# A two-layer MLP by seven products: the first two pairs of up projections interleaved, and the first down loads issued among the last up products

## The chip, the cores and the metric

One NeuronCore of a Trainium2 chip runs the whole program. The metric is device time in microseconds (us), from one launch. TensorE (PE) multiplies, VectorE (DVE), ScalarE (ACT) and GpSimd (POOL) do elementwise work, and the queue of SyncE (SP) issues most DMAs.

## What is computed

The reference is one step of a decoder trunk with two layers. Layer 0 is a pair of state space mixers, layer 1 an attention with three branches, and each layer ends in the same MLP. It runs on 1024 prompt tokens and 8 x 4 sample tokens, 1056 in all:

```python
x += relu(RMSNorm(x) @ w_up)^2 @ w_down      # 1024 -> 4096 -> 1024, once per layer
```

Only the two MLPs are touched. All values are float32.

## The kernel before, in words

**The two MLPs.** Function mlp (L1298) runs once per layer, first on the output of the mixers, then on that of the attention. It has an up stage and a down stage, which follow each other in `R[0], r = W["raw"], ...` to the end of mlp (from L1552).

**Seven products for eight.** Weights and input are each cut into two by two blocks, and a block product is found from seven products p1 to p7 instead of eight (PROD, L1358). p1, p2 and p3 multiply blocks of the input (b11, b21, b22); p5, p6, p7 and p4 multiply sums of blocks (t1, t2, t3, t4). On the weight side a11, a12 and a22 are blocks, s1 to s4 sums of blocks, and p3 uses the sum s4. So p3 has a block of the input but a sum of the weights.

**Split operands.** Each float32 operand is split in two parts, hi and lo. ACT casts hi, DVE subtracts it for lo, and three matmuls (L1372 to L1374, L1513 to L1515) take the place of one. b_split (L1228) splits one input block of 528 columns, prep (L1319) one weight block or sum of 512, two_of (L1423) the operands of down. A product for one pair of weights is 2 column halves x 4 row blocks x 3 = 24 matmuls of 264 columns.

**Up.** There are 16 pairs of weight tiles (index p). up_raw (L1287) loads the raw weights of a pair by two DMAs on SP; sums (L1303) forms s1 to s4 on POOL (L1315); prep splits. The blocks of the input of the first two rows (q = 0, 1) are split and summed while the stage before still runs; those of q = 2, 3 at the start of mlp: b_sum (L1236) forms t1 on DVE and t3, t2, t4 on POOL (L1242), in place in the tiles of the input. The program writes all splits and sums first, then the products of pair 0 (p1, p2, p5, p6, p7, p4), then for each further pair p1, p3 of the pair before, p6, p2, p7, p5, p4. After each product of pair p the weight of the same product of pair p+1 is prepared.

**Evacuation.** p1, p6, p7 and p4 add up in one PSUM bank for each column half (tag A), copied out by ACT after p1, p6 and p7 (L1377) and p4 (L1380). p5 and p3 add up in B, p2 is in C. DVE adds the copies and the banks (L1384, L1388, L1392) and applies relu and square (L1344). t_sums (L1349) forms the sums for down, and everything is stored to DRAM by DMAs on SP (keep, L1339).

**Down.** For each of seven products, 16 steps of 24 matmuls. ready (L1434) issues the loads for one step, a_load (L1409, raw weights) and b_load (L1417, h from DRAM), and the splits. down (L1519) calls ready for three steps before the first and for step i+2 in step i. Before, the first three calls stand behind all products of up.

**What sets the order.** The order in which the program is written is a priority. A scheduler at build time puts each instruction on its engine's queue when, by its own timing, the operands are ready and a buffer is free. Each engine and each queue then works in that order. Buffers are given by tag, with a fixed number each, in the order of the program: "h" 8 (weight sums, raw down weights, p4's copy), "x" 5 (splits of input and of h, t sums), "wh" 4 and "sw" 2 (split weights), "w" 2 and "wr" 2 (raw up weights of even and odd pairs), "e" 12 (evacuated tiles). h tiles of down go to "sw", "w", "wr" in turn (BUF, L1414).

**The sums of squares.** ms_tok (L339) ends the stage before with nine thin matmuls (L343); up starts behind them.

Of the kernel before, what the change touches and what calls it, by code (L numbers as in the profile page):

```python
# [7 lines left out]
F32 = mybir.dt.float32  # L8
# [4 lines left out]
OP = mybir.AluOpType  # L13
# [180 lines left out]
def _build(ctx, nc, tc, ins, outs, dbg):  # L194
    cp = ctx.enter_context(tc.tile_pool(name="consts", bufs=1))
    sp = ctx.enter_context(tc.tile_pool(name="slots", bufs=1))
    phase, psum = [], []
# [18 lines left out]
    cnt = [0]  # L216
# [5 lines left out]
    def wslot(dt, name, tag, bufs):  # L222
        cnt[0] += 1
        return sp.tile([128, 1088], dt, name=f"{name}{cnt[0]}", tag=tag, bufs=bufs)

    def ptile(dt, name, tag, bufs, n=SLOT):

        cnt[0] += 1
        return phase[-1][1].tile([128, n], dt, name=f"{name}{cnt[0]}", tag=tag, bufs=bufs)
# [183 lines left out]
    for c in range(3):  # L413
        cc = slice(c * CH, (c + 1) * CH)
        p = px()
# [812 lines left out]
    def b_split(W, n, q, al=slot):  # L1228

        t, x = al(F32R, "xw"), part(W, n, q)  # L1230
        hi, lo = t[:, :HF], t[:, HF:NT]
        S.copy(hi, x)
        V.tensor_tensor(lo, x, hi.bitcast(F32), OP.subtract)  # L1233
        W["x"][n, q] = hi, lo
# [52 lines left out]
    def up_raw(l, p):  # L1287

        o = []
        for i in range(2):  # L1290
            t = wslot(F32, "wu", "w", 2) if p % 2 == 0 else ptile(F32, "wu", "wr", 2, 1024)
            nc.sync.dma_start(t[:, :1024], ins[f"w_up{l}"][2 * p + i])
            o.append(t[:, :1024].rearrange("p (q k f) -> p k q f", k=2, f=128))
        return o
# [3 lines left out]
    def mlp(l, W, acc, finish, hook=None):  # L1298
# [4 lines left out]
        def sums(p, n):  # L1303

            if (p, n) in SF:
                return SF[p, n]
            (a11, a12), (a21, a22) = [[r[:, k] for k in range(2)] for r in R[p]]
            if n in ("s2", "s4"):
                sums(p, "s1" if n == "s2" else "s2")
            o = half(F32, "sf")  # L1310
            ov = o.rearrange("p (q f) -> p q f", f=128)
            f = lambda k: SF[p, k].rearrange("p (q f) -> p q f", f=128)
            x, y, op = {"s1": lambda: (a21, a22, OP.add), "s2": lambda: (f("s1"), a11, OP.subtract),
                        "s3": lambda: (a11, a21, OP.subtract), "s4": lambda: (a12, f("s2"), OP.subtract)}[n]()
            nc.gpsimd.tensor_tensor(ov, x, y, op)  # L1315
            SF[p, n] = o
            return o

        def prep(p, i):  # L1319

            n = ORDER[i]
            t = wslot(F32R, "sw", "wh", 4) if i < 4 else ptile(F32R, "sw", "sw", 2, 1024)
            hi, lo = t[:, :512], t[:, 512:1024]
            x = sums(p, n) if n[0] == "s" else R[p][int(n[1]) - 1][:, int(n[2]) - 1]
            v = (lambda z: z) if n[0] == "s" else (lambda z: z.rearrange("p (q f) -> p q f", f=128))
            S.copy(v(hi), x)  # L1326
            V.tensor_tensor(v(lo), x, v(hi).bitcast(F32), OP.subtract)
            SW[p, n] = hi, lo

        def e_t():  # L1330
            return ptile(F32, "e", "e", 12, 264)

        def bank(tag, bufs):
            cnt[0] += 1
            return psum[-1][1].tile([128, 512], F32, name=f"{tag}{cnt[0]}", tag=tag, bufs=bufs)[:, :264]

        E = {}

# [3 lines left out]
        def act(x, n, p, c):  # L1342

            V.scalar_tensor_tensor(x, x, 0.0, x, op0=OP.max, op1=OP.mult)  # L1344
            E[p, c, n] = x
            if n != "b12":
                keep(n, p, c, x)

        def t_sums(p, c):  # L1349
# [4 lines left out]
            for n, o, x, y in (("t1", t1, b12, b11), ("t3", b12, b22, b12), ("t2", t2, b22, t1), ("t4", t4, b21, t2)):  # L1354
                V.tensor_tensor(o, x, y, OP.subtract)
                keep(n, p, c, o)

        PROD = {"p1": ("a11", "b11", "A", 1, 0), "p6": ("s2", "t2", "A", 0, 0), "p7": ("s3", "t3", "A", 0, 0),  # L1358
                "p4": ("a22", "t4", "A", 0, 1), "p5": ("s1", "t1", "B", 1, 0), "p3": ("s4", "b22", "B", 0, 1),
                "p2": ("a12", "b21", "C", 1, 1)}  # L1360

        def prod(p, n):
            wn, xn, bk, first, last = PROD[n]
            for c in range(2):
                if first:
                    E[p, c, bk] = bank(bk, 3 if bk == "A" else 2)
                o = E[p, c, bk]
                wh, wl = SW[p, wn]
                for q in range(4):
                    xh, xl = (t[:, c * 264:(c + 1) * 264] for t in W["x"][xn, q])  # L1370
                    a, b = (t[:, q * 128:(q + 1) * 128] for t in (wh, wl))
                    T.matmul(o, a, xh, start=bool(first and q == 0), stop=False, skip_group_check=True)  # L1372
                    T.matmul(o, a, xl, start=False, stop=False, skip_group_check=True)  # L1373
                    T.matmul(o, b, xh, start=False, stop=(q == 3), skip_group_check=True)  # L1374
                if n in ("p1", "p6", "p7"):
                    E[p, c, n] = e_t()
                    S.copy(E[p, c, n], o)  # L1377
                if n == "p4":
                    x = half(F32, "c21")[:, :264]
                    S.copy(x, o)  # L1380
                    act(x, "b21", p, c)
                if n == "p2":
                    x = E.pop((p, c, "p1"))
                    V.tensor_tensor(x, x, o, OP.add)  # L1384
                    act(x, "b11", p, c)
                if n in ("p5", "p7") and (p, c, "B") in E and (p, c, "p7") in E:
                    x = E[p, c, "p7"]
                    V.tensor_tensor(x, x, E[p, c, "B"], OP.add)  # L1388
                    act(x, "b22", p, c)
                if n == "p3":  # L1390
                    x = E.pop((p, c, "p6"))
                    V.tensor_tensor(x, x, o, OP.add)  # L1392
                    act(x, "b12", p, c)
                    t_sums(p, c)
                if last:
                    E.pop((p, c, bk))
            del SW[p, wn]
            if n == "p3":
                del R[p]
            if n == "p5":  # L1400
                prep(p, 6)
            if p < 15 and n != "p3":
                prep(p + 1, ORDER.index(wn))
# [5 lines left out]
        def a_load(i, k, q):  # L1409
# [1 line left out]
            nc.sync.dma_start(t, ins[f"w_dn{l}"][(2 * i + k) * 16 + q])  # L1411
            return t

        BUF = ((lambda: ptile(F32, "br", "sw", 2, 1024)), (lambda: wslot(F32, "br", "w", 2)),  # L1414
               (lambda: ptile(F32, "br", "wr", 2, 1024)))

        def b_load(n, q, o=0, m=HF):  # L1417
            cnt[0] += 1
# [85 lines left out]
        def step(n, q, ops, cs=(0, 1)):  # L1504
            (wh, wl), (xh, xl) = ops
            for dp in range(4):
                a, b = (t[:, dp * 128:(dp + 1) * 128] for t in (wh, wl))
                for c in cs:
# [7 lines left out]
                    if q == 15:  # L1516
                        evac(n, dp, c, o)

        def down():  # L1519
            ks = [(n, q) for n in ("p1", "p5", "p6", "p7", "p3", "p2") + (() if l else ("p4",)) for q in range(16)]  # L1520
            ops = {}
            for i, k in enumerate(ks):
                if k == ("p5", 0):
                    st["r2"] = bcast_tok(r, "r2", xslot(F32, "r2"))
                for z in ([0, 1, 2] if i == 0 else [i + 2]):
                    if z < len(ks):
                        ops[z] = ready(*ks[z])
                step(*k, ops.pop(i))
                after(*k)

                if k[0] in ("p3", "p2", "p4") and (k[1] % 2 or k[0] == "p4"):
                    for _ in range(2 if k[0] == "p4" and k[1] < 4 else 1):
                        if todo:
                            done(todo.pop(0))
# [16 lines left out]

        R[0], r = W["raw"], W["r"]  # L1552
        new_psum("up")
        prep(0, 0)
        sums(0, "s2")
        for q in (2, 3):
            b_split(W, "b11", q, xslot)
        for q in (2, 3):
            b_split(W, "b21", q, xslot if q == 2 else slot)
        prep(0, 2)  # L1560
        for q in (2, 3):
            b_split(W, "b22", q, xslot if q == 2 else slot)
        for q in (2, 3):
            b_sum(W, q, ("t1",), V)
        for n in ("t1", "t3", "t2"):
            if n == "t1":
                for q in (2, 3):
                    b_sum(W, q, ("t3", "t2", "t4"))
            for q in range(4):
                b_split(W, n, q)  # L1570
            prep(0, {"t1": 4, "t3": 1, "t2": 3}[n])
        for q in range(4):
            b_split(W, "t4", q)
        W["a"].clear()
        prep(0, 5)
        V.reciprocal(r, r)
        V.tensor_tensor(r, r, W["m1"], OP.mult)
        R[1] = up_raw(l, 1)
        for n in ("p1", "p2", "p5", "p6", "p7", "p4"):
            prod(0, n)  # L1580
        for p in range(1, 16):
            if p < 15:
                R[p + 1] = up_raw(l, p + 1)
            for n in ("p1", None, "p6", "p2", "p7", "p5", "p4"):
                prod(*((p, n) if n else (p - 1, "p3")))
        prod(15, "p3")
        W["x"].clear()
        new_psum("dn")
# [934 lines left out]
```

## Time and profile before

| | us |
|---|---|
| median of 3 runs | 3127.24 |
| lowest and highest run | 3126.2 and 3130.1 |
| profiled execution | 3129.79 |
| its span, first to last instruction | 3128.0 |
| first MLP, up: first matmul, end | 730.33, about 1075.4 |
| second MLP, up: first matmul, end | 2429.79, about 2774.5 |

The profile is of one execution. Its pages and views give busy time by engine, matmul counts in stretches with the clock that TensorE was granted (1.00 is 2.4 GHz, 0.50 is 1.2 GHz), and each engine's instructions in order of time, with the idle time ahead of one and what ended it. Matmuls overlap: one lasts about 0.28 us, while in a full stretch one starts every 0.12 us. Operations of DVE and ACT overlap a little too, so start-to-start times are used.

### The profile page before, as it was taken

How to read it: one execution, taken by the hardware profiler on the slowest of the kernel's cores; microseconds unless marked ns; L12 is line 12 of the kernel's file. 1: busy time of each engine (PE TensorE's matmuls, PEld its weight loads, DVE VectorE, ACT ScalarE, POOL GpSimd, SP SyncE). 2: the span in 40 equal slices, each digit the busy share in tenths (PEclk: the TensorE clock that was granted, in tenths of full speed). 3: DMA queues.
4: the chain of work that ended last, by engine and by line, in shares of the span. 5: the costliest groups of instructions: out<-in, count | busy, mean ns of one | idle time of the engine just before them, and what ended most of it. 6: DMA issues, size and time to landing. Idle time of an engine off the chain costs nothing. (4 is left out here: it accounts for less than half of the span.)

```text
span 3128.0 us, 58908 instructions
## 1 busy us (share of the span) xinstructions
PE 2970.6 (95%) x22228; PEld 2798.3 (89%) x22228; DVE 2204.7 (70%) x4618; ACT 1412.5 (45%) x2920; POOL 662.9 (21%) x659
## 2 busy tenths in 40 slices
PE   7999998998999999999999989999989899999998
PEld 5999886898999999999999877777869899999998
DVE  5778787778777666866223778777766877757687
ACT  4224565433333344453226666656662433334343
POOL 0000000014222001241001343434332422200133
PEclk8999999998999999999999999999999899999999
DMA  5254444522444584676532121221134344467565
GB/s 187 88 136 136 106 138 118 160 104 96 143 142 146 176 287 130 202 248 192 155 89 76 18 66 45 39 56 38 27 83 137 106 149 144 141 218 244 150 222 159
DMA packets 301285, 414.30 MB, mean 132 GB/s; under 512 B 81012, under 2 KB 202071, under 8 KB 300935
## 3 DMA queue, kind: packets, MB, share of 16 engines
q1 hardware_dynamic: 264640, 340.87, 35.8%
q0 software_dynamic: 20800, 45.43, 5.8%
q10 hardware_dynamic: 15558, 24.22, 2.1%
q8 instruction: 175, 2.87, 0.4%
q14 instruction: 112, 0.91, 0.1%
HBM read 283.81 MB, written 118.18 MB: 129 GB/s over the span
## 5 line engine op out<-in xcount | busy, mean ns | idle before, releaser
L1514 PE MATMUL dn<-xb,sb 128*128 128x264 f32 x1664 | 473.0, 287 | 2.6 <-DVE xb L1427 2.6
L1515 PE MATMUL dn<-xb,sb 128*128 128x264 f32 x1664 | 468.2, 285 | 0.0
L1513 PE MATMUL dn<-xb,sb 128*128 128x264 f32 x1664 | 455.3, 286 | 12.9 <-ACT xb L1426 10.5
L1513 PEld LDWEIGHTS dn<-xb,sb 128*128 128x128 f32 x1664 | 306.8, 189 | 13.5 <-ACT xb L1426 10.9
L1514 PEld LDWEIGHTS dn<-xb,sb 128*128 128x128 f32 x1664 | 315.1, 189 | 3.5 <-DVE xb L1427 3.4
L1515 PEld LDWEIGHTS dn<-xb,sb 128*128 128x128 f32 x1664 | 316.0, 190 | 0.0
L1372 PE MATMUL A<-xw,sw 128*128 128x264 f32 x1024 | 294.8, 289 | 15.9 <-ACT sw L1326 8.5
L1373 PE MATMUL A<-xw,sw 128*128 128x264 f32 x1024 | 294.5, 288 | 3.4 <-DVE xw L1233 3.4
L1374 PE MATMUL A<-xw,sw 128*128 128x264 f32 x1024 | 293.5, 287 | 0.0
L2243 POOL TENSOR_SCALAR P<-P,s,gates 128x640 f32<-128x640 f32 (+7 forms) x256 | 212.2, 843 | 281.0 <-DVE s L2239 231.9
L381 PE MATMUL mm<-xh,wh 128*128 128x352 f32 x672 | 225.4, 336 | 8.1 <-ACT xh L432 7.0
L382 PE MATMUL mm<-xl,wh 128*128 128x352 f32 x672 | 223.4, 333 | 5.3 <-DVE xl L433 5.2
L383 PE MATMUL mm<-xh,wh 128*128 128x352 f32 x672 | 222.6, 331 | 0.0
L2261 DVE TENSOR_TENSOR PT<-px,PT 128x512 fp32r<-128x512 f32 x264 | 177.1, 683 | 53.5 <-ACT PT L2260 52.8
L1372 PEld LDWEIGHTS A<-xw,sw 128*128 128x128 f32 x1024 | 195.6, 192 | 17.5 <-ACT sw L1326 9.0
L2285 PE MATMUL pv<-PT,vs 128*128 128x512 f32 x528 | 195.8, 439 | 11.7 <-ACT PT L2260 6.7
L1373 PEld LDWEIGHTS A<-xw,sw 128*128 128x128 f32 x1024 | 195.4, 191 | 4.1 <-DVE xw L1233 4.1
L2235 ACT ACTIVATE P<-sc,m 128x640 f32<-128x640 f32 (+7 forms) x256 | 180.1, 713 | 41.5 <-DVE m L2229 31.2
L2260 ACT CAST PT<-px 128x512 fp32r<-128x512 f32 x264 | 152.6, 594 | 98.3 <-PE px L2271 97.3
L1374 PEld LDWEIGHTS A<-xw,sw 128*128 128x128 f32 x1024 | 196.1, 192 | 0.0
L2215 PE MATMUL sc<-KT,qt 128*128 128x256 f32 x1216 | 193.6, 298 | 0.0
L2229 DVE TENSOR_REDUCE m<-sc 128x1 f32<-128x640 f32 (+7 forms) x176 | 167.0, 949 | 30.9 <-PE sc L2215 26.9
(652 smaller groups left out, 8465.6 us busy)
## 6 DMA issues: line engine op xcount, KB each, us to landing
ar<-i_w_dn SPq DMA_DIRECT2D x256, 256.0 KB
wu<-i_w_up SPq DMA_DIRECT2D x64, 512.0 KB
br<-h0t_d SPq DMA_DIRECT2D x64, 264.0 KB
wr<-i_w_in_e POOLq DMA_DIRECT2D x26, 512.0 KB, 4.5
h0t_d<-ts SPq DMA_DIRECT2D x96, 132.0 KB
br<-h0b_d SPq DMA_DIRECT2D x48, 264.0 KB
h1t_d<-ts SPq DMA_DIRECT2D x96, 132.0 KB
br<-h1b_d SPq DMA_DIRECT2D x48, 264.0 KB
```

What stands on the lines that cost most here:

```text
L381: T.matmul(o, wh, xh, start=(j == 0), stop=False)
L382: T.matmul(o, wh, xl, start=False, stop=False)
L383: T.matmul(o, wl, xh, start=False, stop=(j == n - 1))
L1372: T.matmul(o, a, xh, start=bool(first and q == 0), stop=False, skip_group_check=True)
L1373: T.matmul(o, a, xl, start=False, stop=False, skip_group_check=True)
L1374: T.matmul(o, b, xh, start=False, stop=(q == 3), skip_group_check=True)
L1513: T.matmul(o, a, h, start=(q == 0), stop=False)
L1514: T.matmul(o, a, g, start=False, stop=False)
L1515: T.matmul(o, b, h, start=False, stop=(q == 15))
L2215: T.matmul(p[:, c:c + n], w_, t, start=first, stop=True, skip_group_check=True)
L2243: nc.gpsimd.tensor_scalar(P, P, b["s"][:, h:h + 1], GT[:, qb, gc:gc + 1], op0=OP.mult, op1=OP.mult)
L2285: T.matmul(PV[g, qb, i], v, t, start=(a == 0 and kb == 0 and k == 0), stop=False)
```

## The change

At the start of up, pair 1's raw weights are loaded first, and the products of pairs 0 and 1 alternate, written out by hand: p1, p2, p3 of pair 0, the same of pair 1, then p5, p6, p7 and p4, each of both pairs. The splits and sums stand between them, each ahead of the product that needs it. For these two pairs weight sums run on DVE, and all sums of the input's blocks at q = 2, 3 run on DVE. p3 of these pairs has a bank of its own and is copied out by ACT; DVE adds copy and bank after p6. Pair 2's weights are prepared before p7 and p4 of these pairs end; from pair 2 on the order is as before. The banks are four of tag A and four that B and C share, the evacuated tiles are 15. The row factors r are inverted later.

At the end of up, ready is called for the first three steps of down, ahead of p7, p5 and p4 of pair 15. The splits of the input are let go after their last product, and h tiles take the buffers "w", "wr", "sw" in turn.

```diff
-            nc.gpsimd.tensor_tensor(ov, x, y, op)
+            (V if p < 2 else nc.gpsimd).tensor_tensor(ov, x, y, op)
...
-            return ptile(F32, "e", "e", 12, 264)
+            return ptile(F32, "e", "e", 15, 264)
...
-            return psum[-1][1].tile([128, 512], F32, name=f"{tag}{cnt[0]}", tag=tag, bufs=bufs)[:, :264]
+            return psum[-1][1].tile([128, 512], F32, name=f"{tag}{cnt[0]}", tag=tag, bufs=4)[:, :264]
...
             wn, xn, bk, first, last = PROD[n]
+            if p < 2 and n == "p3":
+                bk, first = "C", 1
             for c in range(2):
                 if first:
-                    E[p, c, bk] = bank(bk, 3 if bk == "A" else 2)
+                    E[p, c, bk] = bank("A" if bk == "A" else "B")
...
-                if n in ("p1", "p6", "p7"):
+                if n in ("p1", "p6", "p7") or p < 2 and n == "p3":
                     E[p, c, n] = e_t()
                     S.copy(E[p, c, n], o)
...
+                if p < 2 and n == "p6":
+                    x = E.pop((p, c, "p6"))
+                    V.tensor_tensor(x, x, E.pop((p, c, "p3")), OP.add)
+                    V.tensor_tensor(x, x, E[p, c, "B"], OP.add)
+                    act(x, "b12", p, c)
...
             del SW[p, wn]
+            if p == 15:
+                for q in range(4):
+                    del W["x"][xn, q]
...
-        BUF = ((lambda: ptile(F32, "br", "sw", 2, 1024)), (lambda: wslot(F32, "br", "w", 2)),
-               (lambda: ptile(F32, "br", "wr", 2, 1024)))
+        BUF = ((lambda: wslot(F32, "br", "w", 2)), (lambda: ptile(F32, "br", "wr", 2, 1024)),
+               (lambda: ptile(F32, "br", "sw", 2, 1024)))
...
+R[1] = up_raw(l, 1)
 prep(0, 0)
-sums(0, "s2")
 for q in (2, 3): b_split(W, "b11", q, xslot)
 for q in (2, 3): b_split(W, "b21", q, xslot if q == 2 else slot)
 prep(0, 2)
+prod(0, "p1")
+for n in ("s1", "s2", "s4"): sums(0, n)
+prep(0, 6)
 for q in (2, 3): b_split(W, "b22", q, xslot if q == 2 else slot)
+prod(0, "p2"); prep(1, 0); prod(0, "p3"); prep(1, 2)
+for n in ("s1", "s2", "s4"): sums(1, n)
+prep(1, 6); prod(1, "p1")
 for q in (2, 3): b_sum(W, q, ("t1",), V)
+for q in range(4): b_split(W, "t1", q)
+prep(0, 4); prod(1, "p2"); prep(1, 4); prod(1, "p3")
-(t3, t2, t4 of q = 2, 3 on POOL; splits of t1, t3, t2, t4; then up_raw(l, 1) and all products of pair 0)
+for q in (2, 3): b_sum(W, q, ("t3", "t2"), V)
+for q in range(4): b_split(W, "t2", q)
+prod(0, "p5"); prep(0, 1); prep(1, 1); prod(1, "p5"); prep(0, 3)
+for q in range(4): b_split(W, "t3", q)
+prod(0, "p6"); prep(1, 3); prep(0, 5); prod(1, "p6")
+for q in (2, 3): b_sum(W, q, ("t4",), V)
+for q in range(4): b_split(W, "t4", q)
+prep(1, 5); R[2] = up_raw(l, 2)
+prod(0, "p7"); prep(2, 0); prep(2, 1); prod(1, "p7"); prep(2, 2); prep(2, 3)
+prod(0, "p4"); prod(1, "p4"); prep(2, 4); prep(2, 5)
-for p in range(1, 16):
+for p in range(2, 16):
...
             for n in ("p1", None, "p6", "p2", "p7", "p5", "p4"):
-                prod(*((p, n) if n else (p - 1, "p3")))
+                if p == 15 and n in ("p7", "p5", "p4"):
+                    z = ("p7", "p5", "p4").index(n)
+                    ops[z] = ready(*ks[z])
+                if n:
+                    prod(p, n)
+                elif p > 2:
+                    prod(p - 1, "p3")
```

(The start is written here with several calls on a line, and one line in brackets stands for the old order.)

## Rows read from the trace of the kernel before

**Rows 1.** The page's first part: busy us, share of the span, instructions.
```profile
PE 2970.6 (95%) x22228; PEld 2798.3 (89%) x22228; DVE 2204.7 (70%) x4618; ACT 1412.5 (45%) x2920; POOL 662.9 (21%) x659
```

**Rows 2.** Windows, PE alone: stretch and length, busy (matmuls), granted clock, DMA share, GB/s.
```profile
730.33:770.00 39.67, 29.67 (x185) 0.78 0.17 57
770.00:1060.00 290.00, 290.00 (x2382) 1.00 0.45 144
2429.79:2470.00 40.21, 30.47 (x190) 0.79 0.11 35
...
1070.00:1100.00 30.00, 23.17 (x176) 0.89 0.90 286
2770.00:2800.00 30.00, 25.85 (x187) 0.89 0.88 295
1100.00:1130.00 30.00, 30.00 (x248) 1.00 0.67 211
```

**Rows 3.** Timeline of PE, start of up: start, us, instruction [idle before <- releaser].
```profile
745.19 0.59 PE L1372 MATMUL A<-xw,sw 128*128 128x264 f32 x1 [4.79 <-ACT sw L1326]
...
762.32 0.59 PE L1372 MATMUL A<-xw,sw 128*128 128x264 f32 x1 [1.90 <-ACT e L1377]
```

**Rows 4.** Waits, 730 to 770: total us, times, longest.
```profile
ACT xw L1232 <- POOL xa L1242: 8.5, 3, 5.6
```

**Rows 5.** Timeline of POOL, start of the first up.
```profile
721.64 1.29 POOL L1315 TENSOR_TENSOR sf<-wu,wu 128x512 f32<-128x512 f32 x1 [0.46 <-DVE acc L1207]
...
732.19 9.95 POOL L1315 TENSOR_TENSOR sf<-wu 128x512 f32<-128x512 f32 x1 [7.01 <-DMA wu<-i_w_up]
...
746.27 5.20 POOL L1242 TENSOR_TENSOR xa<-xa,xa 128x528 f32<-128x528 f32 x3
```

**Rows 6.** Timeline of DVE: input splits during and after that POOL operation.
```profile
738.47 2.55 DVE L1233 TENSOR_TENSOR xw<-xa,xw 128x528 fp32r<-128x528 f32 x4
...
748.73 3.32 DVE L1233 TENSOR_TENSOR xw<-xa,xw 128x528 fp32r<-128x528 f32 x2 [0.15 <-ACT xw L1232]
```

**Rows 7.** Windows of 2 us: PE, PEld, DVE, ACT, POOL busy (counts), granted clock, DMA share, GB/s.
```profile
732.00:734.00 2.00, 2.00 (x11) 2.00 (x11) 2.00 (x5) 2.00 (x5) 1.81 (x1) 0.50 0.94 380
...
750.00:752.00 2.00, 2.00 (x11) 2.00 (x10) 2.00 (x3) 1.42 (x3) 2.00 (x2) 0.50 0.00 0
```

**Rows 8.** Timeline of PE: two neighbours at the lower clock.
```profile
732.33 0.42 PE L1372 MATMUL C<-xw,sw 128*128 128x264 f32 x1
732.55 0.42 PE L1373 MATMUL C<-xw,sw 128*128 128x264 f32 x1
```

**Rows 9.** Timeline of DVE: neighbours of 264 columns.
```profile
771.25 0.43 DVE L1355 TENSOR_TENSOR e<-e,e 128x264 f32<-128x264 f32 x1
771.59 0.43 DVE L1355 TENSOR_TENSOR ts<-e,ts 128x264 f32<-128x264 f32 x1
```

**Rows 10.** Groups by line, DVE, 730.33 to 770: count, busy, mean ns, idle before.
```profile
L1233 DVE TENSOR_TENSOR xw<-xa,xw 128x528 fp32r<-128x528 f32 x21 | 19.6, 963 | 3.3 <-ACT xw L1232 3.2
```

**Rows 11.** Timeline of SP's queue at the end of the first up.
```profile
1063.21 7.66 SPq L1340 DMA_DIRECT2D h0b_d<-e  x4
...
1072.28 0.43 SPq L1411 DMA_DIRECT2D ar<-i_w_dn  x1
1072.80 1.32 SPq L1420 DMA_DIRECT2D br<-h0b_d  x1
```

**Rows 12.** Timeline of ACT, same place.
```profile
1081.02 0.62 ACT L1426 CAST sb<-ar 128x512 fp32r<-128x512 f32 x1 [1.93 <-DMA ar<-i_w_dn]
1081.54 1.70 ACT L1426 CAST xb<-br 128x528 fp32r<-128x528 f32 x3
```

**Rows 13.** Timeline of PE: first matmuls of the two down stages.
```profile
1082.22 2.13 PE L1513 MATMUL dn<-xb,sb 128*128 128x264 f32 x8 [6.83 <-ACT xb L1426]
...
2778.17 1.23 PE L1513 MATMUL dn<-xb,sb 128*128 128x264 f32 x8 [3.63 <-ACT xb L1426]
```

**Rows 14.** Timeline of DVE: the last p3 of the first up taken from its bank.
```profile
1077.19 0.42 DVE L1392 TENSOR_TENSOR e<-e,B 128x264 f32<-128x264 f32 x1
```

More of the change, by code (lines that the diff above doesn't have):

```diff
@@ L1330, in e_t, with bank @@
         def e_t():
-            return ptile(F32, "e", "e", 12, 264)
-        def bank(tag, bufs):
+            return ptile(F32, "e", "e", 15, 264)
+        def bank(tag):
             cnt[0] += 1
-            return psum[-1][1].tile([128, 512], F32, name=f"{tag}{cnt[0]}", tag=tag, bufs=bufs)[:, :264]
+            return psum[-1][1].tile([128, 512], F32, name=f"{tag}{cnt[0]}", tag=tag, bufs=4)[:, :264]
         E = {}
@@ L1381, in prod @@
                     act(x, "b21", p, c)
+                    if p < 2:
+                        t_sums(p, c)
                 if n == "p2":
@@ L1385, in prod @@
                     act(x, "b11", p, c)
+                if p < 2 and n == "p6":
[3 more added lines that the diff above has]
+                    act(x, "b12", p, c)
                 if n in ("p5", "p7") and (p, c, "B") in E and (p, c, "p7") in E:
-                    x = E[p, c, "p7"]
+                    x = E.pop((p, c, "p7"))
                     V.tensor_tensor(x, x, E[p, c, "B"], OP.add)
                     act(x, "b22", p, c)
-                if n == "p3":
+                    if p < 2:
+                        E.pop((p, c, "B"))
+                if p >= 2 and n == "p3":
                     x = E.pop((p, c, "p6"))
@@ L1397, in prod @@
             del SW[p, wn]
+            if p == 15:
+                for q in range(4):
+                    del W["x"][xn, q]
+            if p < 2:
+                return
             if n == "p3":
@@ L1517, in step @@
                         evac(n, dp, c, o)
+        ks = [(n, q) for n in ("p1", "p5", "p6", "p7", "p3", "p2") + (() if l else ("p4",)) for q in range(16)]
+        ops = {}
         def down():
-            ks = [(n, q) for n in ("p1", "p5", "p6", "p7", "p3", "p2") + (() if l else ("p4",)) for q in range(16)]
-            ops = {}
             for i, k in enumerate(ks):
@@ L1525, in down @@
                 for z in ([0, 1, 2] if i == 0 else [i + 2]):
-                    if z < len(ks):
+                    if z < len(ks) and z not in ops:
                         ops[z] = ready(*ks[z])
@@ L1560, in mlp @@
         prep(0, 2)
+        prod(0, "p1")
+        for n in ("s1", "s2", "s4"):
+            sums(0, n)
+        prep(0, 6)
         for q in (2, 3):
             b_split(W, "b22", q, xslot if q == 2 else slot)
+        prod(0, "p2")
+        prep(1, 0)
+        prod(0, "p3")
+        prep(1, 2)
+        for n in ("s1", "s2", "s4"):
+            sums(1, n)
+        prep(1, 6)
+        prod(1, "p1")
         for q in (2, 3):
             b_sum(W, q, ("t1",), V)
[L1565 to L1571, printed above, removed]
+        for q in range(4):
+            b_split(W, "t1", q)
+        prep(0, 4)
+        prod(1, "p2")
+        prep(1, 4)
+        prod(1, "p3")
+        for q in (2, 3):
+            b_sum(W, q, ("t3", "t2"), V)
+        for q in range(4):
+            b_split(W, "t2", q)
+        prod(0, "p5")
+        prep(0, 1)
+        prep(1, 1)
+        prod(1, "p5")
+        prep(0, 3)
+        for q in range(4):
+            b_split(W, "t3", q)
+        prod(0, "p6")
+        prep(1, 3)
+        prep(0, 5)
+        prod(1, "p6")
+        for q in (2, 3):
+            b_sum(W, q, ("t4",), V)
         for q in range(4):
@@ L1574, in mlp @@
         W["a"].clear()
-        prep(0, 5)
+        prep(1, 5)
+        R[2] = up_raw(l, 2)
+        prod(0, "p7")
+        prep(2, 0)
+        prep(2, 1)
+        prod(1, "p7")
+        prep(2, 2)
+        prep(2, 3)
+        prod(0, "p4")
         V.reciprocal(r, r)
         V.tensor_tensor(r, r, W["m1"], OP.mult)
-        R[1] = up_raw(l, 1)
-        for n in ("p1", "p2", "p5", "p6", "p7", "p4"):
-            prod(0, n)
-        for p in range(1, 16):
+        prod(1, "p4")
+        del R[0], R[1]
+        prep(2, 4)
+        prep(2, 5)
+        for p in range(2, 16):
             if p < 15:
```

## The prediction

> **What bounds the kernel now.** The page's first part comes first: PE is busy for 95% of the span [rows 1], so time can only be won where PE stands or runs slow, and the place of each stretch counts, not a share. Next, a windows view of PE alone [rows 2]. In the middle of the up stage of the first MLP 2382 matmuls take 290.00 us, 0.1217 us each, which I take for the second MLP too. Around that, four stretches are thinner. From the first up matmul at 730.33 to 770 there are 185 matmuls, 183 of them up products (two belong to the row sums): at 0.1217 they need 22.3 us of the 39.67, so 17.4 are lost. In the second MLP 190 matmuls need 23.1 of 40.21 us: 17.1 lost. Where up hands over to down, 176 and 187 matmuls lie in 30 us, where the down stage a little later has 248 (0.121 each): 8.7 and 7.4 us lost. Together 50.6 us; all that the change can return lies in there.
>
> What ends the idle times at the start is read on PE's timeline [rows 3]: 4.79 us until ACT's cast of a weight tile, 1.90 until an evacuation. Those casts stand in ACT's queue behind casts of the sums t3, t2 and t4, which wait for POOL: 8.5 us in three waits [rows 4]. POOL's timeline says why it is late [rows 5]: a weight sum that takes 1.29 us with little beside it lasted 9.95 us from 732.19, with DVE at work back to back, and the block sums after it took some 1.7 each (three in 5.20). DVE pays as well [rows 6]: four splits of 528 columns took 2.55 us (0.64 each) while that one stood, two took 3.32 (1.66 each) beside the sums after it. So the start hangs on POOL and DVE hindering each other, while PE has pair 0 alone to work on. Each pause has a price behind it: at a granted clock of 0.50 (1.2 GHz) [rows 7], matmuls start 0.22 us apart [rows 8], 0.098 more than at full clock.
>
> **The change, part by part: the start.** Pairs 0 and 1 alternate: p1, p2, p3 of each need only block splits of the input, then p5, p6, p7, p4, which need t1 to t4. That gives PE 2 x 3 x 24 = 144 matmuls (17.5 us) before the first t, where now it has 48 of p1 and p2 and then p5. All t sums of the last two rows of blocks and all weight sums of pairs 0 and 1 go to DVE. Off POOL: six block sums and eight weight sums per MLP. Does DVE carry it? I count its work from the first matmul to p6 of pair 2, the first product that needs a POOL sum. Large operations: 5 splits of b11, b21, b22; 8 weight sums; 8 block sums; 16 splits of t; 12 weight splits: 49 x 0.64 = 31.4. Small ones of 264 columns, which start 0.34 us apart [rows 9]: p2 two, p6 three (one more than now, since p3 is added from a copy), p7 two, for two pairs and two column halves: 28 x 0.345 = 9.7. Two weight splits of pair 2: 1.3; the row factors 0.5. Sum 42.9 us. PE needs 15 products of 24 x 0.1217 = 2.92, so 43.8, and about 1.5 for the opening dip of the clock that is there today and stays (0.50 from 732 to 734 [rows 7], behind the thin row sums ahead of it): 45.3. DVE has 2.4 us to spare.
>
> Two things eat that. Pair 2's four weight sums stay on POOL and fall into this window, after the raw weights of pair 2 arrive, whose buffer is free only when a22 of pair 0 is split. While POOL works, a DVE operation costs 1.0 us more; I take 0.8 for each POOL operation: 3.3. And DVE waits in order for ACT's casts, 3.3 us in the present window [rows 10]; I take 3.0 again. 2.4 - 6.3 = 3.9 us late. Behind such a pause I count 14 matmuls at 0.22: 1.4. So each start keeps 1.5 + 5.3 = 6.8 and returns 17.4 - 6.8 = 10.6 and 17.1 - 6.8 = 10.3. Bounds: it keeps 1.5 alone if DVE is never late; no more than now is the other end, unless the clock goes (below).
>
> Edits costed at nothing: four more ACT copies of p3 and A and B banks at four each (PE has no wait for a bank in the steady stretch, so nothing to win); the load of pair 1's weights issued before the splits; the 20 operations of p4's evacuation and the t sums (20 x 0.345 = 6.9 us), which are covered by pair 2's products, since nothing reads them before down; without that cover they would come on top. The stores on SP's queue move with them. The weight sums of pair 0 on DVE lie partly before the first matmul, where DVE has gaps.
>
> **The end of up.** Now the first weight load of down stands on SP behind four stores that hold it from 1063.21 for 7.66 us, goes out at 1072.28, and the third operand's h load at 1072.80 [rows 11]. ACT casts the third weight at 1081.02 and only then, in its order, the first h tile at 1081.54 [rows 12]; PE starts at 1082.22 after 6.83 us, in the second MLP after 3.63 [rows 13]. The change puts each of the first three pairs of loads and casts ahead of p7, p5, p4 of pair 15, some 12, 9 and 6 us before the end, and gives the first h load the buffers of even weight pairs, free since pair 14. The splits take the input's buffers that p1 and p2 of pair 15 have let go. Six loads pass stores of pair 15 on SP; behind those wait only e tiles, of which there are 15 now. Each SP entry takes about 0.4 us. ACT's evacuation copies of p7 and p4 now stand behind casts that may wait for a load; the three products left, 8.8 us, cover that. The handover is bounded below by nothing (down has none inside) and above by today's. What is late next is DVE's evacuation of the last p3 at 1077.19 [rows 14], some 2 us after its product, whose bank a dn tile reuses. I keep 1.5 each: 8.7 - 1.5 = 7.2 and 7.4 - 1.5 = 5.9.
>
> **Sum.** 10.6 + 10.3 + 7.2 + 5.9 = 34.0 us. Off the profiled execution (3129.79 us, of which 3128.0 span) that is 3095.8; the median of the runs is 2.55 lower, so 3093.
>
> **Rivals.** First, *POOL is shut out* by a DVE that never rests. For it: the 9.95 us [rows 5], over while DVE next idled. Against: DVE has waits in its order, and POOL passes in them, as in its three sums in 5.20. Price: POOL begins pair 2 when DVE has drained, 42.9 + 6.9 + 1.3 = 51.1 us after the first matmul; two sums, a cast and a split, 4.6 more: 55.7 instead of 45.3, 10.4 late, and 30 slow matmuls, 2.9. Each start keeps 14.8, returns 2.6 and 2.3, with the ends 18.0: 3109. The Trainium skill, page "SBUF — State Buffer", section "Who interferes with whom", has such a rule: a DVE operation with two SBUF inputs and a POOL operation that reads SBUF exclude each other, and the later one waits for the whole of the first. By it this rival would be the likeliest; the trace agrees for the 9.95 us, but not for the stretch after it, where both advanced.
>
> Second, *the loads don't come earlier*: the order within an engine is set by a scheduler and by free buffers, and the third load's buffers are free only after p4. Then the ends return nothing: 3127.2 - 20.9 = 3106. For it: those stores on SP. Against: the first pair alone lets PE start, and its buffers are free.
>
> Third, *slower: the clock stays down*. If DVE feeds PE in small portions over all of pairs 0 and 1, PE may stay at 0.50: 336 matmuls x 0.22 = 73.9 us. Now they end 39.67 + 153 x 0.1217 = 58.3 us after the first one. 15.6 later in each MLP, less 13.1 at the ends: +18, 3145. It decides from 175 slow matmuls per start (10.6 + 6.5 us over 0.098). For it: after 745 the clock was still 0.50 at 750 to 752 with PE at work all that time [rows 7]. Against: it came back during p1 to p3, and the first six products have operands in time. The Trainium skill, "TensorE: Matmul & The Clock Gate", section "A second HAM failure mode: psum-queue depth-cycling", tells of a kernel whose short pauses between groups of matmuls cost it the clock again and again; by it, this rival would hold; the trace shows two such falls in a start, not a lasting one.
>
> **The numbers.** Runs lie 0.12% apart, and 0.2% (6 us) is what can be told from no change. Forecast 0.62, POOL shut out 0.18, no earlier loads 0.09, clock 0.05, and 0.06 that the parts cancel. Faster takes the first three, less 0.01: 0.88; same 0.06; slower is the clock and that 0.01. The range begins where each start keeps 1.5 and the ends nothing, 50.6 - 3.0 = 47.6, near 3080, and ends beyond the two milder rivals, at 3113.
>
> **What would show it.** Right: six products back to back from the first matmul, block and weight sums of L1242 and L1315 on DVE at 0.64, POOL empty until pair 2; less than 2 us before the first dn matmul, with its weight load issued before the last p7 ends. Wrong: PE waiting on DVE splits of t with the clock at 0.50 through most of pairs 0 and 1; a POOL sum of pair 2 of 8 us or more with p6 waiting; a dn matmul that still waits for an xb cast.

## The result and the profile after

Four runs gave a median of 3096.1 us (3094.2 to 3100.8), beside them the kernel before 3127.6: a ratio of 0.9904 with an interval of 0.9891 to 0.9917: some 31 us or 1% faster. The forecast was 3093, its range 3080 to 3113. The profiled execution took 3094.23 us, its span is 3092.4 (3128.0 before).

PE's windows first, as in [rows 2]: stretch and length, busy (matmuls), granted clock, DMA share, GB/s. The first and third begin at the first up matmul, the next two lie where up hands over to down.

```profile
731.72:771.40 39.68, 39.68 (x312) 0.96 0.28 88
...
2404.65:2444.86 40.21, 38.65 (x300) 0.96 0.23 70
1055.00:1085.00 30.00, 27.77 (x228) 1.00 0.79 268
2733.00:2763.00 30.00, 28.76 (x236) 1.00 0.85 286
1075.00:1105.00 30.00, 30.00 (x248) 1.00 0.79 274
```

The starts hold 312 and 300 matmuls where they held 185 and 190. At 0.1217 us each they lose 39.68 - 38.0 = 1.7 and 40.21 - 36.5 = 3.7 us (17.4 and 17.1 before). A window counts every matmul that lies in it in part, two too many here, so these losses are some 0.3 us too small; by starts, from the first up matmul to the 311th, they are 2.1 and 4.2. The handovers lose 20 and 12 matmuls against 248, 2.4 and 1.5 us (8.7 and 7.4 before).

What PE waited for from the first up matmul on is read in the list of its waits (total us, times, longest), first up to 800:

```profile
PE B L1378 <- DVE sw L1327: 1.4, 1, 1.4
PE A L1377 <- DVE xw L1233: 0.2, 1, 0.2
```

No cast and no POOL sum stands ahead of PE there any more, as it did in [rows 3, 4]. One wait comes later, at 819, and on the way to it DVE stands for a store:

```profile
819.44 0.39 PE L1378 MATMUL B<-xw,sw 128*128 128x264 f32 x1 [1.20 <-DVE sw L1327]
```

```profile
812.75 1.27 DVE L1355 TENSOR_TENSOR ts<-e,e 128x264 f32<-128x264 f32 x1 [2.56 <-DMA h0t_d<-ts]
```

The second up, from 2404.6 to 2500, is not as clean; each start also has its opening dip of the clock (0.55 and 0.60 from 732 to 736 in the first).

```profile
PE B L1378 <- DVE sw L1327: 3.1, 1, 3.1
PE A L1376 <- ACT e L1381: 1.3, 1, 1.3
PE A L1378 <- DVE sw L1327: 0.2, 1, 0.2
```

The 3.1 us stand at 2474, behind the first window, inside p3 of pair 2, which reads s4. DVE's timeline says why the split was late (start, us, instruction, idle before and its releaser):

```profile
2461.93 0.69 DVE L1327 TENSOR_TENSOR sw<-wu,sw 128x512 fp32r<-128x512 f32 x1
2467.86 0.43 DVE L1355 TENSOR_TENSOR ts<-e,e 128x264 f32<-128x264 f32 x1 [5.25 <-DMA h1t_d<-ts]
...
2470.27 1.65 DVE L1327 TENSOR_TENSOR sw<-sf,sw 128x512 fp32r<-128x512 f32 x1
2471.84 0.42 DVE L1344 SCALAR_TENSOR_TENSOR e<-e 128x264 f32<-128x264 f32 x1
2472.18 1.75 DVE L1327 TENSOR_TENSOR sw<-sf,sw 128x512 fp32r<-128x512 f32 x1
```

A t sum writes into a buffer whose earlier contents are still on their way to memory; it stands 5.25 us for that store, and everything on DVE stands behind it, the split of s4 among it. POOL, which the trace shows idle for 12.44 us until the same store, then ran further weight sums beside the splits (1.65 and 1.75 us instead of 0.68). After PE's pause the clock was at 0.50 for about 5 us:

```profile
2472.00:2474.00 2.00, 0.02 (x1) 0.75 0.20 68
2474.00:2476.00 2.00, 2.00 (x9) 0.50 0.23 72
2476.00:2478.00 2.00, 2.00 (x11) 0.50 0.43 144
2478.00:2480.00 2.00, 2.00 (x12) 0.55 0.52 175
2480.00:2482.00 2.00, 2.00 (x19) 1.00 0.25 87
```

At the end of up the loads go out early: the first weight loads of down leave SP at 1041.48, where the first left at 1072.28 in [rows 11], six h loads have left by 1054.22, and the first down product follows the last up product directly.

```profile
1041.48 1.41 SPq L1429 DMA_DIRECT2D ar<-i_w_dn  x3
```

The second down bank still waits, as PE's timeline and then DVE's show:

```profile
1065.12 0.28 PE L1533 MATMUL dn<-xb,sb 128*128 128x264 f32 x1
1067.63 0.39 PE L1531 MATMUL dn<-xb,sb 128*128 128x264 f32 x1 [2.23 <-DVE e L1405]
```

```profile
1066.53 0.71 DVE L1445 TENSOR_TENSOR xb<-br,xb 128x528 fp32r<-128x528 f32 x1 [1.31 <-ACT xb L1444]
1067.15 0.42 DVE L1405 TENSOR_TENSOR e<-e,B 128x264 f32<-128x264 f32 x1
```

The evacuation of the last p3 (that of [rows 14]) stands behind the split of the third step's h tile, whose cast waited 3.33 us for its load; that load had its buffer only after p4 and left SP at 1062.14, behind five stores.

### The profile page after: what moved, and what is told of

It is laid out like the page before. It is cut to its first block, busy times and chain, and to the rows that moved or that the text cites. A ratio compares the mean times of both kernels' runs of the same rounds, so it can differ in the third digit from the quotient of the medians.

```text
span 3092.4 us, 58900 instructions
## 1 busy us (share of the span) xinstructions
PE 2953.1 (95%) x22228; PEld 2783.7 (90%) x22228; DVE 2203.0 (71%) x4654; ACT 1409.7 (46%) x2928; POOL 611.2 (20%) x631
## 5 line engine op out<-in xcount | busy, mean ns | idle before, releaser
L1376 PE MATMUL A<-xw,sw 128*128 128x264 f32 x1024 | 290.4, 286 | 1.4 <-ACT e L1381 1.3
L1377 PE MATMUL A<-xw,sw 128*128 128x264 f32 x1024 | 291.4, 286 | 0.2 <-DVE xw L1233 0.2
L1378 PE MATMUL A<-xw,sw 128*128 128x264 f32 x1024 | 290.8, 285 | 0.2 <-DVE sw L1327 0.2
L1378 PE MATMUL B<-xw,sw 128*128 128x264 f32 x768 | 218.0, 286 | 5.7 <-DVE sw L1327 5.7
L1377 PE MATMUL B<-xw,sw 128*128 128x264 f32 x768 | 219.7, 286 | 0.0
L1376 PE MATMUL B<-xw,sw 128*128 128x264 f32 x768 | 219.5, 286 | 0.0
L1376 PEld LDWEIGHTS A<-xw,sw 128*128 128x128 f32 x1024 | 192.9, 190 | 2.0 <-ACT e L1381 1.6
L1378 PEld LDWEIGHTS A<-xw,sw 128*128 128x128 f32 x1024 | 194.1, 190 | 0.4 <-DVE sw L1327 0.4
```

## The experiments

To compare kernels without the parts that vary by chance, I use a **mark**: the time from the first up matmul to the 49th down matmul (the third down step's first), both by their starts, once per MLP. It holds a whole up stage and its handover; unhindered it would be 2688 x 0.1217 + 48 x 0.121 = 332.9 us. All runs, each ratio beside the kernel before on the same chip:

| kernel | median us | ratio, interval | mark 1 | mark 2 |
|---|---|---|---|---|
| before | 3127.2 | | 359.7 | 357.9 |
| changed | 3096.1 | 0.9904, 0.9891 to 0.9917 | 341.5 | 345.1 |
| changed, second chip | 3102.1 | 0.9916, 0.9900 to 0.9933 | 342.3 | 343.9 |
| changed, third chip | 3104.1 | 0.9916, 0.9900 to 0.9932 | 342.6 | 344.0 |
| new start alone | 3109.7 | 0.9940, 0.9923 to 0.9956 | 348.2 | 349.5 |
| early loads alone | 3118.5 | 0.9972, 0.9959 to 0.9984 | 354.3 | 352.3 |
| t sums in place | 3098.0 | 0.9909, 0.9892 to 0.9926 | 341.1 | 341.4 |
| pair 2's sums on DVE | 3093.9 | 0.9900, 0.9880 to 0.9919 | 338.1 | 339.7 |
| third load elsewhere | 3099.2 | 0.9911, 0.9890 to 0.9931 | 342.0 | 344.3 |
| new order, sums on POOL | 3108.4 | 0.9942, 0.9923 to 0.9961 | 347.8 | 350.0 |
| old order, sums on DVE | 3121.2 | 0.9970, 0.9955 to 0.9984 | 354.0 | 351.7 |
| banks rotated | 3101.7 | 0.9903, 0.9883 to 0.9924 | 342.8 | 344.0 |
| three edits | 3098.4 | 0.9894, 0.9875 to 0.9913 | 339.9 | 339.0 |
| banks swapped | 3090.0 | 0.9879, 0.9862 to 0.9895 | 337.4 | 337.9 |

**Changed, second chip** (no edit).

> The changed kernel once more, for a second profile and on the same chip as the next three. If both ends of up bring the gain, the up stages and handovers repeat to within 1 us: first matmul to first dn matmul 333 and 338 us, about 29 us less than before in the two together; then the 8.7 us that the attention was shorter in the first profile are chance and may be gone. If part of the gain is made in the attention, by an order that the change moved there, its 599 us (score matmuls, first to last) come back too, and the median stays near 3096.

The gain is 26 us on this chip, 28 on the third (whose median, 3104.1, lies above the 3096 to 3102 expected below) and 31 on the first, while the marks agree within 1.3 us. What varies beside them is above all the attention between the two MLPs, where the change moves nothing: 598.8 us in the first profile of the changed kernel, 604.0 and 607.1 in the others, 607.4 before.

**New start alone**: the three early `ready` calls are left out.

```diff
-                if p == 15 and n in ("p7", "p5", "p4"):
-                    z = ("p7", "p5", "p4").index(n)
-                    ops[z] = ready(*ks[z])
```

> The changed kernel with down's loads issued behind all products of up, as before; the rest of the change stays. Parts that add up: the prediction put the ends at 13.1 us and the starts at 20.9, so this one is near 3109, some 13 us above the changed kernel, with waits of 4 to 7 us before the first dn matmul. If the loads come no earlier for being written earlier: within 3 us of the changed kernel.

**Early loads alone**: the kernel before with these lines, the buffer order and the early release of the input's tiles.

> The kernel before with only the end of the change: ready for three steps of down among the products of pair 15, the order of the buffers, and the splits let go early. Parts that add up: 3127 less 13, near 3114, and less than 2.5 us of wait in one piece at the handover. If the early loads collide with the stores of pair 15: no faster than 3124.

Marks: the start returns 11.5 and 8.4 us, the loads 5.4 and 5.6; added, 16.9 and 14.0, where both together return 17.1 to 18.2 and 12.8 to 14.0. The parts add up. In times, 18.6 and 9.9 (13 expected) stand against 26.3 for both on this chip. The loads do come earlier: with them the wait before down fell from 6.83 us [rows 13] to 1.8, on DVE's evacuation; without them it stayed at 6.8.

**T sums in place**: t1 and t2 overwrite b11 and b22, and t4 takes an e tile; the buffer with the late store goes.

```diff
-            t = xslot(F32, "ts")
-            t1, t2, t4 = (t[:, i * 264:(i + 1) * 264] for i in range(3))
-            for n, o, x, y in (("t1", t1, b12, b11), ("t3", b12, b22, b12), ("t2", t2, b22, t1), ("t4", t4, b21, t2)):
+            t4 = e_t()
+            for n, o, x, y in (("t1", b11, b12, b11), ("t3", b12, b22, b12), ("t2", b22, b22, b11), ("t4", t4, b21, b22)):
```

> The changed kernel with the sums t1 and t2 of t_sums written in place into evacuated tiles that were stored long before, and t4 into an evacuated tile, so that no buffer of tag x has to wait for a store. Theory: in the second start DVE stood 5.25 us for such a store, pair 3's weight sums stood behind it, and PE then waited 3.10 us and ran some 8 us at half clock; that goes, the second up gets 5 to 7 us shorter, the first 0 to 2, and the time is near 3090. Rival: POOL's sums for pairs 2 and 3 beside DVE are the cause; then the 3 us wait of PE stays and the time is within 2 us of the changed kernel.

PE's waits in the second up, 2404 to 2500 (the px row lies ahead of the first up product):

```profile
PE A L1375 <- ACT e L1380: 2.0, 1, 2.0
PE px L343 <- DVE acc L1252: 1.3, 1, 1.3
PE A L1376 <- DVE xw L1233: 0.8, 1, 0.8
PE B L1377 <- DVE sw L1327: 0.3, 1, 0.3
```

The 3.1-us wait is gone, DVE waits for no store of ts, and mark 2 is 2.5 to 3.7 us shorter, less than the 5 to 7 expected, mark 1 as before. So the stall came with that buffer; the gain in time can't be told from none.

**Pair 2's sums on DVE.**

```diff
-            (V if p < 2 else nc.gpsimd).tensor_tensor(ov, x, y, op)
+            (V if p < 3 else nc.gpsimd).tensor_tensor(ov, x, y, op)
```

> The changed kernel with pair 2's four weight sums on DVE as well, so that POOL stands empty until pair 3. Theory (what is left at the start of up is DVE's own queue, above all its stand for a store under the t sums, and not POOL beside it): DVE takes over 4 x 0.64 = 2.6 us and is spared the slowed operations beside POOL (768.19 to 772.48 in the first up, some 2 us); first up 332 to 334 us as in the changed kernel (333.2 and 332.7), second up stays at 335 to 338 with its wait of some 3 us, time within 4 us of the changed kernel. Rival (what is left is DVE and POOL hindering each other over pair 2): the 3.1-us wait of the second up goes, second up 333, time 3 to 6 us less than the changed kernel's.

My theory fell, at least in size. Mark 1 is 3.4 to 4.5 us shorter, mark 2 4.2 to 5.4 (the intervals of the ratios still overlap), and in the first up PE's list has one row left:

```profile
PE A L1377 <- DVE xw L1233: 0.2, 1, 0.2
```

So in the first up the wait of 1.4 us came from DVE and POOL at work together over pair 2. In the second up the wait on that split falls to 1.6 us although the t sums keep their buffer. It is not relief from POOL there: DVE still stands for the store, 4.27 us, and the two splits behind it still take 1.67 and 1.75. Against the first up matmul its stand ends 3.3 us earlier; what brought that forward isn't shown.

**Third load elsewhere**: that step's h tile takes a buffer of pair 14's weights.

```diff
-            t = BUF[q % 3]()
+            t = BUF[0 if (n, q) == ("b11", 2) else q % 3]()
```

> The changed kernel with the third down step's block loaded into the buffer ring of pair 14's weights, free long before, and so not behind p4's last product and four stores on SP. Theory (the 2.2 us before the second dn bank are DVE's: the last p3's evacuation stands behind a split of the third step, whose load is late): that split leaves DVE's tail, the evacuation of the last p3 starts within 1 us of its last matmul instead of 2.4, and the waits on DVE before the first dn matmuls fall from 2.1 and 2.0 us to under 1 in both MLPs; time 1 to 3 us under the changed kernel's, which these rounds may not tell. Rival (the dn banks wait for DVE whatever stands ahead, because its small operations of p7, p4 and p3 are late there): waits stay at 1.5 to 2.3.

The wait stayed, 2.6 and 1.4 us. DVE's timeline at the first handover:

```profile
1066.97 0.69 DVE L1445 TENSOR_TENSOR sb<-ar,sb 128x512 fp32r<-128x512 f32 x1 [1.84 <-ACT sb L1444]
1067.59 0.43 DVE L1355 TENSOR_TENSOR ts<-e,e 128x264 f32<-128x264 f32 x1
1067.93 0.42 DVE L1405 TENSOR_TENSOR e<-e,B 128x264 f32<-128x264 f32 x1
```

The third step's split is out of the way, and the fourth's weight split stands in its place, late for the same reason. The edit took away one late load, not the place behind late loads, so it parts neither theory from the other.

**New order, sums on POOL**: weight sums of pairs 0 and 1 and t3, t2, t4 back on POOL.

> The changed kernel's order with the weight sums of pairs 0 and 1 and the block sums t3, t2 and t4 back on POOL, as in the kernel before; six products of two pairs still stand ahead of the first t. Theory (POOL beside a DVE that works back to back is what makes the start slow, and the new order needs the sums off it): p3 needs s4, the third sum of a chain, as early as the third product, one POOL sum of 4 to 10 us is enough to stop PE there, and four or more such sums stand in line; up to half of the gain is left, first up 340 to 352 us (changed kernel 333), time 3110 to 3127. Rival (the order alone gives the gain, by its distance between product and sum): first up 333 to 336, time within 5 us of the changed kernel's.

**Old order, sums on DVE**: the kernel before with those sums on DVE.

> The kernel before, its order unchanged, with the weight sums of pairs 0 and 1 and the block sums t3, t2 and t4 on DVE. Theory (both halves are needed: off POOL the sums are quick, but with pair 0 alone PE has two products, 5.8 us, before DVE must have finished t1's sums and splits): DVE has some 25 large operations of 0.64, 16 us, in front of p6 of pair 0, so PE still stands; first up 341 to 347 us instead of 351.9, time 3106 to 3120. Rival (the moved sums are the whole gain): first up 333 to 336, time 3104 or less, the kernel that has the new start alone being 3109.7. The other rival (the order is the whole gain): first up 349 to 353, time 3124 to 3130.

The new order alone, against the early loads alone, returns 354.3 - 347.8 = 6.5 and 352.3 - 350.0 = 2.3; the moved sums alone, against before, 5.7 and 6.2; both, 11.5 to 12.8 and 7.2 to 8.4. Neither is the whole and neither is nothing: both rivals fall, and the halves all but add. Both times lie 1 to 2 us outside what each theory gave, 3108.4 below its range and 3121.2 above. In the run with the sums on POOL, POOL's timeline again has a weight sum that lasts, and PE then waits 3.2 us for an evacuation that stands behind casts of POOL's sums:

```profile
734.19 7.31 POOL L1315 TENSOR_TENSOR sf<-wu 128x512 f32<-128x512 f32 x1 [10.93 <-DMA wu<-i_w_up]
741.47 1.78 POOL L1242 TENSOR_TENSOR xa<-xa,xa 128x528 f32<-128x528 f32 x1
```

```profile
PE B L1376 <- ACT e L1381: 3.2, 1, 3.2
PE B L1376 <- DVE e L1390: 1.8, 2, 0.9
```

**Banks rotated**: the down stage asks for its eight banks at once and begins with the third.

```diff
+            B8 = [dn()[:, :264] for _ in range(8)] if q == 0 and len(cs) == 2 else None
...
-                        PS[dp, c] = dn()[:, :264]
+                        PS[dp, c] = B8[(2 * dp + c + 2) % 8] if B8 else dn()[:, :264]
```

> The changed kernel, with the eight PSUM banks of the down stage handed out from the third on, so that the two that the last p3 of up leaves are written seventh and eighth in a step and not first and second. Theory (the wait before the second dn bank is nothing but that bank's late evacuation): DVE's tail stays as it is, its last evacuation still about 2.4 us behind its matmul; the first dn products of six banks, 6 x 0.365 = 2.2 us, run meanwhile, and the waits of 2.0 to 2.6 us in the first MLP and 1.2 to 2.0 in the second fall to under 0.6; time 2 to 4 us under the changed kernel beside it. Rival (the down stage's second and third operands are late as well, by the late load and the late splits, and PE only waits there instead): the waits move to an xb or sb split before the second or third step, sum unchanged.

The wait stayed (2.3 and 1.5 us), after three down matmuls as before: the edit did nothing. As I read the built program, a bank is given at its first use, so the order was 0, 7, 6, 5 as ever, and the last p3's banks are 5 and 7; the traces don't number the banks. This run is one more of the changed kernel.

**Three edits** (in place, pair 2 on DVE, rotated banks) and **changed, third chip**, side by side.

> The changed kernel with three edits: the t sums in place, without the buffer whose store DVE waited for; pair 2's weight sums on DVE; the down stage's banks handed out from the third on. Theory (the three remove waits in places of their own): first up 329 to 331 us, second up 330 to 333, both handovers without a wait over 0.6; 6 to 10 us under the changed kernel beside it. Rival (the t sums in place and pair 2's sums on DVE mend one and the same stall, of the splits of p5 in pair 2): second up stays at 332 to 334, 3 to 6 us under it.

> The changed kernel as it is, beside the two others on the same chip: 3096 to 3102, first up 333, second up 336 to 338, waits of 2.0 to 2.6 and 1.2 to 2.0 us before the second dn bank. A first up or a handover that differs by over 1.5 us from its two earlier profiles would show that differences of that size between profiles say nothing.

3091.3 to 3100.0 against 3103.4 to 3104.8: the three edits are faster, by 5.7 us between the medians, with waits at the handovers as before. Since the rotation did nothing, this is the gain of the first two. Against pair 2's sums alone (338.1 and 339.7) the t sums in place add nothing in the first MLP (1.8 us longer) and 0.7 us in the second (332.4 to 331.7 from the first up matmul to the first down matmul): the two mostly mend one stall, as the rival has it. The time is the rival's too; the second up's 331.7 lies in the theory's range and just under the rival's.

**Banks swapped**: the first two edits, and one bank of the second group asked for first, so that the groups change places.

```diff
         R[1] = up_raw(l, 1)
-
+        bank("B")
```

> The t sums in place and pair 2's weight sums on DVE, as in the kernel with all three edits; and the handover's banks tried again. In the two kernels with the banks rotated the down stage still used them in the order 0, 7, 6, 5, since a bank is given at the first use and not where it is asked for: the two that the last p3 leaves were still among the first four (7 was second). Here the up stage's two groups of banks change places, by one bank of the second group asked for and never used; the last p3's second half then lies in bank 3, sixth in a down step, its first half in bank 1, eighth. Theory (only the late evacuation of that bank): no wait before the second bank; five banks, 5 x 0.365 = 1.8 us, run first, and some 0.3 to 1.0 us before the sixth is left of 2.1 in the first MLP, under 0.5 of 1.1 to 1.5 in the second; first up 329 to 331 us, second 330 to 332. Rival (an operand of a later step is late as well): the wait moves to the second or third step, and the time from the first up matmul to the 49th dn matmul is no shorter than in the kernel with all three edits.

PE's first handover; five banks are filled before the wait, not one:

```profile
1060.06 0.28 PE L1530 MATMUL dn<-xb,sb 128*128 128x264 f32 x1
...
1063.17 0.39 PE L1530 MATMUL dn<-xb,sb 128*128 128x264 f32 x1 [1.11 <-DVE e L1404]
```

1.1 us is left of 2.1 in the first MLP, 0.2 of 1.1 in the second, and from the first down matmul to the mark both are 1.0 us shorter than with three edits: the wait was that bank and nothing behind it. (Mark 1 is 2.5 us shorter; its other 1.5 lie in up, before the handover.) At 3090.0 us and a ratio of 0.9879 (0.9862 to 0.9895) this kernel has the lowest ratio, its interval clear of the changed kernel's on the second and third chips, though it overlaps the first one's and that of the three edits.

## Why the prediction was right

**The sum.** The four terms gave 34.0 us; the marks moved by 18.2 + 12.8 = 31.0 (31.4 and 31.0 in the other two profiles). The mechanism holds, and the sum is 3 us too large. The measured time moved by 31, 26 and 28 us. In the first profile the attention happens to be 8.6 us shorter, so part of the nearness of 3096.1 to 3093 is luck. Against that the second down stage is longer: from its mark to the end 340.3 us before, 342.6, 343.7 and 344.4 after. It is lost at a wait that the trace of before has not, at the first product of the last p4, and behind it:

```profile
3028.68 0.36 PE L1531 MATMUL dn<-sb,a 128*128 128x264 f32 x1 [1.73 <-DVE Y L1506]
```

It is 1.7 to 2.1 us in the three profiles of the changed kernel, in two of them with the clock at 0.50 behind it; the hundred matmuls around it lose 2.8, 4.0 and 3.9 us against 0.1 before. The wait is absent with either part alone, though with the new start alone 1.6 us are lost there too. So by these profiles 2.3 to 4.1 us were given back later, which no step foresaw; what makes that evacuation late, I did not try.

The terms can be set against what PE lost by starts: a stretch's time less 0.1217 for each matmul in it. From the first up matmul to the last that is 17.8 and 17.5 us before, 6.0 and 10.6 in the first profile after (5.5 and 8.7, 5.7 and 9.2 in the others). In the first profile the first start returned 1.1 more than forecast, the second 3.5 less, the ends 0.7 less together: the sum is nearer than its worst term.

**The first start** was forecast at 10.6 and returned 11.7 (12.2 and 12.0 in the others). It kept 6.0, near the 6.8 forecast, but made up otherwise: 2.1 in the window, 2.2 with the 1.4-us wait, and 1.5 at 819 behind the store, which the prediction has no term for (with the t sums in place that stretch loses 0.1). The term that was mis-sized is ACT's 3.0 us of waits in DVE's order. The groups of DVE by line, from the first up matmul to 771.4, show no idle time ahead of any split (count, busy us, mean ns, idle before):

```profile
L1233 DVE TENSOR_TENSOR xw<-xa,xw 128x528 fp32r<-128x528 f32 x21 | 15.2, 744 | 0.0
```

In [rows 10] it was 3.3 with 963 ns of mean. With slack 2.4 and POOL's 3.3 alone, DVE would be 0.9 us late; PE waited 1.4. POOL's price was well set: of the small operations and the split beside its four sums, 1.21, 1.18, 1.79 and 1.51 us, some 3.7 are excess.

**The second start** was forecast at 10.3 and returned 6.8 (8.8 and 8.2): 4.2 lost in the window, some 6 with the pause, which are its 3.1 us and the low clock behind it, with 28 matmuls from 2474 to 2480 where 49 fit. Here ACT's waits were there (4.0 us), and the step that failed is the t sums "costed at nothing ... covered by pair 2's products". I had named the cover of their 6.9 us of work, but not the store that the buffer's next writer waits for.

**The ends** were forecast at 7.2 and 5.9 and returned 6.4 and 6.0 (5.1 and 5.2, 5.0 and 5.7 in the others). What is late next was named rightly, the last p3's evacuation, at 2.2 and 1.2 us instead of 1.5; that a late load's split would stand ahead of it was not. One reading was off: by the old buffer order the h load that left SP at 1072.80 is the first step's, which goes to "sw", and not the third's; the new order gives that step a buffer that is free earlier, as the forecast has it.

**The rivals.** POOL was not shut out: its first sum of pair 2 ran at 767.82, 36 us after the first matmul, in 1.29 us; in the second MLP it took 3.64 us at 2438.33, short of the 8 that would have decided. The Trainium skill's rule ("SBUF — State Buffer", "Who interferes with whom") fits the trace both ways, also beside POOL sums in a row, the kind of stretch that the prediction held against it. In the first up DVE's slowed operations end 0.3 to 0.6 us after a POOL sum does, as if they waited for the whole of it, and the one among them that reads bank B took 0.42 (POOL's lines, then DVE's):

```profile
767.82 1.29 POOL L1315 TENSOR_TENSOR sf<-wu 128x512 f32<-128x512 f32 x1 [77.71 <-DMA wu<-i_w_up]
769.18 1.36 POOL L1315 TENSOR_TENSOR sf<-sf,wu 128x512 f32<-128x512 f32 x1
```

```profile
768.19 1.21 DVE L1344 SCALAR_TENSOR_TENSOR e<-e 128x264 f32<-128x264 f32 x1
769.32 0.42 DVE L1399 TENSOR_TENSOR e<-e,B 128x264 f32<-128x264 f32 x1
```

The sums of 3.64 and 7.31 us end 1.2 us after DVE begins an operation that reads a bank (2440.73, 740.28), the one of 9.95 [rows 5] 1.1 us after DVE's row of splits ended. The loads came earlier. The clock did not stay down: from 736 on it was 1.00 through pairs 0 and 1, against the slower rival and the Trainium skill's case beside it ("TensorE: Matmul & The Clock Gate", "A second HAM failure mode: psum-queue depth-cycling"); behind the opening dips it fell once in that profile's up stages, behind the 3.1-us pause.

## What to carry to other kernels

At a stage's start, put first the work that needs the least preparation, of two units and not of one, and take preparation off an engine that is slowed beside a busy one; here each was worth about half in the first MLP, and in the second the moved sums were worth more (6.2 us against 2.3). Before moving an operation on an in-order engine, ask what its output buffer waits for as well as its inputs: one store's landing stopped every split behind it. Where a stage hands its accumulator banks to the next, let the next write the last-freed bank last, and look in the built program at which bank that is.

## What the runs showed of the hardware that was not expected

- Pauses of nearly one length left the clock in different states. At the first handover a wait of 2.23 us was followed by 1.00 in the changed kernel's first profile; in its third, a wait of 2.10 us by 0.50 (1066 to 1068), which cost 9.7 - 8.3 = 1.4 us from the first down matmul to the mark. Over the runs with the early loads, waits there of 1.80, 2.06, 2.10 and 2.27 us were followed by 0.50, and waits of 1.92, 1.94, 2.14, 2.23 and 2.63 us were not. PE's windows of the changed kernel on the third chip:

```profile
1064.00:1066.00 2.00, 0.84 (x5) 0.86 1.06 393
1066.00:1068.00 2.00, 2.00 (x11) 0.50 1.03 344
1068.00:1070.00 2.00, 2.00 (x15) 0.78 1.05 382
```

- One kind of POOL sum, 128x512, took 1.29 to 1.75 us in the first up although DVE worked beside it, and DVE paid with operations of 1.2 to 1.8 us instead of 0.42 or 0.69. In the second up it took 3.64 and with the sums on POOL 7.31 (9.95 in [rows 5]); there DVE's operations kept to 0.42 and 0.69 nearly to the end. Each of these three came in only where DVE read a bank or stood idle. With both queued on operands outside the banks, the two took turns in the first up, and POOL stood through ten DVE operations with the sums on POOL; what decides between these stayed open.
- The attention stage, untouched by any edit, took from 598.8 to 608.4 us in fourteen profiles: more than several of the effects looked for here.
